# Sums of squares one group later, M products behind the state products, and scores one query behind

## The chip, the cores and the metric

One core of one Trainium2 chip. The metric is the device time of one execution in microseconds; smaller is better.

## What is computed

One layer of a hybrid encoder block over 1024 tokens of width 1024: attention and a bidirectional Mamba-2 mixer side by side, gates, then an expert mixer (PEER) whose experts are picked by product keys. Two places matter here. In the Mamba-2 mixer each chunk of 128 tokens gets, per group of 8 heads, a product with a decay matrix, a product with the running state, and then a norm over the whole width:

```python
y_diag = jnp.einsum('bgrcls,bcsgrp->bclgrp', cb[:, :, None] * Lmat, X)
y_off = jnp.einsum('bclgn,bcgrpn,bgrcl->bclgrp', Cc, states, jnp.exp(A_cs))
...
y = y_f + y_b + xh * d_skip.astype(jnp.float32).reshape(G, R)[:, :, None]
return rmsnorm(y * jax.nn.silu(z), ssd_norm_w)
```

In PEER every token gets 16 queries (8 heads, two halves); each is scored against 128 keys, and the 16 best are kept:

```python
q = (xt @ w_query).reshape(T, PEER_HEADS, 2, PEER_D_HALF)
s1 = jnp.einsum('thd,hkd->thk', q[:, :, 0], keys1).astype(jnp.float32)
v1, i1 = lax.top_k(s1, PEER_TOPK)
```

## The kernel before

The kernel is one long program in stages. Large matmuls are done as three passes over rounded high parts and remainders (`mm3`, L209 to L211), so one product over 8 tiles of the contraction is 24 matmuls. In most stages a scheduler of the framework orders each engine's instructions and gives out the buffers when the program is built; on the chip each engine then runs its own list strictly in that order.

**The state-space stage** (from `discretize`, L689, to L868). A first loop over chunks 7 to 1 makes the backward states. The second loop over chunks 0 to 7 calls `outputs(c, ...)`, which handles two groups of 8 heads, g = 0 and 1. Per group: POOL writes four masked tiles `r0h, r0l, r1h, r1l` (L796); PE multiplies them (L802), ACT takes the exponential `E` (L804); POOL and DVE build `M` from `cb` and `cu` (L806, L809) and multiply it with `E` (L811); PE multiplies `M` with the chunk's tokens `xk` into a PSUM tile `y` (L815, "the products with M"). PE spreads the decays over 128 rows (L820), ACT copies them to `de` (L824), PE multiplies the states `St` and `Sb` (L830, "the state products"). DVE joins all to `yt` (L832 to L840), multiplies it with the gate `zt` loaded from DRAM (L843); the result is stored, ACT squares it into `zt` (L845), and PE sums the squares over the rows with four matmuls (L849) into `oq`. After the second group ACT copies the sums to `ysum` (L852).

`oq` and `cu` share one PSUM bank: `cu` is its second half, and DVE's step L809 reads it. `oq`, `y` and four other short-lived tiles of a chunk come from the same three banks (`C1`, tag `pb`). `step(FSTEP)` ends a group with two pieces of other work that is ready, the filler: columns of the input projection, later of the attention's up projection. A piece is 24 or 12 matmuls into the single bank `w`, with weights split by ACT (L179) and POOL (L180). The scheduler spreads filler between the group's steps on PE. The filler is used up before the last chunks.

**The query loop** (L1112 to L1120) is behind the attention's and mixer's output product. For each of 16 query tiles m: 24 matmuls with 384 columns give the first 384 tokens' queries in PSUM, ACT copies them to `q` (L1083), PE scores them against the keys with three matmuls (`score`, L1093), ACT copies the scores to `s` (L1094), and DVE picks the 16 best of each of three blocks (`top`, L1101 to L1105). The normalising of the other 640 tokens runs beside it (`normed`, L1031, L1033, and its splits at L179 and L180). After the loop the order on PE, DVE and POOL is written out by hand: routing of the three blocks (`route`, with an exponential at L1180), hidden products of the experts (`hb`, gelu at L1459), the other tokens' queries, and then the expert stages up to the end.

Of the kernel before, what the change touches and what calls it, by code (L numbers as in the profile page):

```python
# [10 lines left out]
F32 = mybir.dt.float32  # L11
# [13 lines left out]
NB = -(-TB // 128)  # L25
# [99 lines left out]
def block(ctx, tc, A, out, dbg=None):  # L125
    nc = tc.nc
    dbg = dbg or {}
    V, ACT, PE, POOL = nc.vector, nc.scalar, nc.tensor, nc.gpsimd
# [22 lines left out]
    one = ka[:, K_ONE:K_ONE + 128]  # L151
# [150 lines left out]
    r = rstd(p0, acc, S, 1.0 / D)  # L302
# [313 lines left out]
    def C1():  # L616
        return psC.tile([128, 512], F32, name="pb", bufs=4 - NW)
# [15 lines left out]
    ss = pool("ss")  # L633
# [50 lines left out]
    def step(k):  # L684
        nonlocal steps
        for _ in range(min(k, steps - KEEP)):
            steps -= 1
            next(filler, None)
# [53 lines left out]
    def states(c, d, xc, xk):  # L742
        o = C1()
        for g in range(2):
            PE.transpose(o[:, g * 128:(g + 1) * 128], xc[:, 8 + g], ident)
        bk = ss.tile([128, 256], F32, name="bk")
        ACT.copy(bk, o[:, :256])
        xd = ss.tile([128, D], F32, name="xd")
        POOL.tensor_tensor(xd.rearrange("p (h d) -> p h d", h=16), xk.rearrange("p (h d) -> p h d", h=16),
                           dd[:, c, 16 * d:16 * d + 16].unsqueeze(2).to_broadcast([128, 16, 64]), op=OP.mult)  # L750
        o = C2()
        for g in range(2):
            PE.matmul(o[:, g], lhsT=bk[:, g * 128:(g + 1) * 128], rhs=xd[:, g * 512:(g + 1) * 512], start=True, stop=True)
        return o

    def advance(src, o, c, d):
        dst = ss.tile([128, D], F32, name="St", bufs=2)
        if src is None:
            ACT.copy(v2(dst), o)
            return dst  # L760
        t = ss.tile([128, D], F32, name="adv")
        V.tensor_tensor(t.rearrange("p (h d) -> p h d", h=16), src.rearrange("p (h d) -> p h d", h=16),
                        tot[:, c, 16 * d:16 * d + 16].unsqueeze(2).to_broadcast([128, 16, 64]), op=OP.mult)
        V.tensor_tensor(v2(dst), o, v2(t), op=OP.add)
        return dst

    def outputs(c, xc, xk, Sf):
# [22 lines left out]
        for g in range(2):  # L790
# [9 lines left out]
            for j in range(2):  # L800
                for i, (w, r) in enumerate(R):
                    PE.matmul(o[:, j], lhsT=w, rhs=r[:, 4 * j:4 * j + 4], start=(i == 0), stop=(i == 3))  # L802
            E = ss.tile([128, 8, 128], F32, name="E")
            ACT.activation(E.rearrange("p (s h) l -> p s (h l)", s=2), o, AF.Exp)  # L804
            M = ss.tile([128, 8, 128], F32, name="M", bufs=2)
# [3 lines left out]
                V.scalar_tensor_tensor(M[:, r], cu[:, g], dt[:, c, 8 * g + r:8 * g + r + 1], M[:, r],  # L809
                                       op0=OP.mult, op1=OP.add)  # L810
            V.tensor_tensor(M, M, E, op=OP.mult)  # L811
            y = C1()
            for r in range(8):
                h = 8 * g + r
                PE.matmul(y[64 * (r % 2):64 * (r % 2) + 64, (r // 2) * 128:(r // 2 + 1) * 128],  # L815
                          lhsT=xk[:, h * 64:(h + 1) * 64], rhs=M[:, r], start=True, stop=True, skip_group_check=True)
            od = C2()
            for d in dirs:
                for j in range(4):
# [6 lines left out]
            for d in dirs:  # L826
                st = (Sf, Sb)[d]
                for j in range(4):
                    hs = slice((8 * g + 2 * j) * 64, (8 * g + 2 * j + 2) * 64)
                    PE.matmul(of[:, d, j * 128:(j + 1) * 128], lhsT=st[:, hs], rhs=xc[:, 10 + g],  # L830
                              start=True, stop=True, skip_group_check=True)
            V.tensor_tensor(de[:, ds], of[:, ds], de[:, ds], op=OP.mult)  # L832
            yt = ss.tile([128, 4, 128], F32, name="yt", bufs=2)
            ytf = yt.rearrange("p a l -> p (a l)")
# [3 lines left out]
            for j in range(4):  # L838
                m = 4 * g + j
                V.scalar_tensor_tensor(yt[:, j], xc[:, m], cols[:, C_DS + m:C_DS + m + 1], yt[:, j], op0=OP.mult, op1=OP.add)  # L840
            zt = ss.tile([128, 4, 128], F32, name="zt")
            nc.sync.dma_start(zt, z_d[:, 4 * g:4 * g + 4, cl_(c)])
            V.tensor_tensor(yt, yt, zt, op=OP.mult)  # L843
            nc.sync.dma_start(y_d[:, 4 * g:4 * g + 4, cl_(c)], yt)
            ACT.activation(zt, yt, AF.Square)  # L845
            if g == 0:
                qr = slice(32 * (c // 2), 32 * (c // 2) + 32)
            for j in range(4):
                PE.matmul(oq[qr, :128], lhsT=one[:, 0:32], rhs=zt[:, j], start=(g == 0 and j == 0),  # L849
                          stop=(g == 1 and j == 3))  # L850
            step(FSTEP)
        ACT.copy(ysum[qr, (c % 2) * 128:(c % 2) * 128 + 128], oq[qr, :128])  # L852

    def cl_(c):
        return slice(c * 128, (c + 1) * 128)
# [9 lines left out]
    for c in range(8):  # L865
        xc, xk = tokens(c)
        outputs(c, xc, xk, Sf)
        if c < 7:  # L868
            Sf = advance(Sf, states(c, 0, xc, xk), c, 0)
    step(10 ** 6)  # L870
    ss.release()
    psC.release()
# [234 lines left out]
    def new_q():  # L1107
        return sp.tile([128, S], F32, name="q", bufs=2)

    norm = normed(ends[1], accs[1])  # L1110
    next(norm)
    for m in range(16):  # L1112
        q = new_q()
        for _ in query(weights(A["wq"][m], 8), q, CUTS[:1]):
            pass
        if m % 2 or not m:
            next(norm)
        s = score(m, q, range(NB))
        for b in range(NB):
            top(m, s[:, b], b)  # L1120

    psD.release()
    psE = pool("psE", space=PSUM)
# [743 lines left out]
```

## Time and profile before

| | us |
|---|---|
| runs of the kernel | 3949.39, 3956.99, 3957.73; median 3956.99 |
| the profiled execution | 3962.2 |
| its span in the trace | 3960.4 |
| state-space outputs, first to last L802/L849 | 690 to 1043 of the span |
| query loop | 1284 to 1386 of the span |

The profile is one execution on the chip. Engines: PE is the matmul engine, PEld its weight loads, DVE the vector engine, ACT the scalar engine, POOL GpSimd, SP the queue of DMA issues. A line such as L849 is the line of the kernel that issued the instruction. "Idle before" an instruction is time in which its engine stood still, with what ended it. Matmuls with 32-bit operands stand as two rows each in the trace's counts, so four of them read x8. [...]

### The profile page before, as it was taken

Reading aid. Unit: us, or ns where it says so; the run is one execution under the profiler, and the core shown is the slowest. Engines: PE = TensorE matmul, PEld = TensorE weight load, DVE = VectorE, ACT = ScalarE, POOL = GpSimd, SP = SyncE. Lnnn points to the kernel's source line nnn. Section 1 sums busy time; section 2 is a strip of 40 time slices with the busy share of each in tenths; the row PEclk is TensorE's granted clock in tenths of the full one; section 3 lists DMA queues with packets and bytes.
Section 4 is the critical chain, followed back from the end, with each engine's and each line's share of the span. In section 5 each row is a group of like instructions: output and inputs, shape, how many; then the busy total and the mean of one; then the engine's idle time right before and its main releaser. Section 6 shows DMA issues by size and latency. Waiting matters only on the chain. (4 is left out here: it accounts for less than half of the span.)

```text
span 3960.4 us, 61117 instructions
## 1 busy us (share of the span) xinstructions
PE 3631.6 (92%) x22927; PEld 3189.8 (81%) x22927; DVE 2574.5 (65%) x5289; ACT 1356.3 (34%) x2672; POOL 1803.3 (46%) x1526
## 2 busy tenths in 40 slices
PE   7999999988889899999889798699999999999998
PEld 4777767766679799987678698697888999888997
DVE  5788831457672678787875567594447898545556
ACT  5455532223323433322236465222122222222222
POOL 3111122566454567778775456444443444444200
PEclk9999999998899999999999899799999999999999
DMA  5111134233375258877767778888887888888632
GB/s 197 47 46 48 55 117 144 92 106 101 122 241 168 94 201 317 311 284 258 244 231 273 264 265 320 310 300 303 322 323 246 295 297 292 310 317 314 236 117 81
DMA packets 387064, 852.32 MB, mean 215 GB/s; under 512 B 32720, under 2 KB 146896, under 8 KB 384080
## 3 DMA queue, kind: packets, MB, share of 16 engines
q1 hardware_dynamic: 276176, 445.72, 32.9%
q0 software_dynamic: 110592, 402.70, 28.7%
q8 instruction: 180, 2.95, 0.3%
q14 instruction: 116, 0.95, 0.1%
HBM read 739.70 MB, written 108.59 MB: 214 GB/s over the span
## 5 line engine op out<-in xcount | busy, mean ns | idle before, releaser
L209 PE MATMUL hb<-ah,wh 128*128 128x320 f32 x2048 | 653.2, 319 | 24.0 <-ACT a L1459 24.0
L211 PE MATMUL hb<-ah,wl 128*128 128x320 f32 x2048 | 641.1, 313 | 9.7 <-POOL wl L199 9.7
L210 PE MATMUL hb<-al,wh 128*128 128x320 f32 x2048 | 639.9, 312 | 0.0
L1282 POOL DMA_INDIRECT br<-u,bidx x384 | 370.3, 964 | 369.0 <-DVE br L1314 243.2
L199 POOL TENSOR_TENSOR wl<-wr,wh 128x512 fp32r<-128x512 f32 x269 | 352.9, 1317 | 397.3 <-ACT wh L198 367.6
L209 PE MATMUL pb<-Wh,vh 128*128 128x320 f32 x1536 | 477.1, 317 | 57.1 <-ACT Wh L1689 33.7
L180 POOL TENSOR_TENSOR wl<-wr,wh 128x512 fp32r<-128x512 f32 x172 | 233.0, 1358 | 615.5 <-ACT wh L179 450.6
L1282 POOL DMA_INDIRECT br<-v,ixt x384 | 376.8, 981 | 267.5 <-PE gx L1361 155.1
L210 PE MATMUL pb<-Wl,vh 128*128 128x320 f32 x1536 | 481.4, 314 | 1.7 <-DVE Wl L1692 1.6
L211 PE MATMUL pb<-Wh,vl 128*128 128x320 f32 x1536 | 479.6, 313 | 0.0
L1314 DVE SCALAR_TENSOR_TENSOR br<-br,gx 128x1024 f32<-128x1024 f32 x384 | 454.0, 1214 | 8.6 <-DMA br<-u,bidx 6.3
L209 PEld LDWEIGHTS hb<-ah,wh 128*128 128x128 f32 x2048 | 391.9, 191 | 52.7 <-ACT a L1459 28.2
L211 PEld LDWEIGHTS hb<-ah,wl 128*128 128x128 f32 x2048 | 390.7, 191 | 11.3 <-POOL wl L199 10.3
L210 PEld LDWEIGHTS hb<-al,wh 128*128 128x128 f32 x2048 | 391.5, 191 | 0.0
L1722 DVE TENSOR_TENSOR acc<-acc,pb 128x320 f32<-128x320 f32 x491 | 230.6, 485 | 222.2 <-PE pb L211 221.0
L179 ACT CAST vh<-vr 128x512 fp32r<-128x512 f32 x256 | 151.1, 618 | 649.8 <-PE pb L210 449.0
L209 PEld LDWEIGHTS pb<-Wh,vh 128*128 128x128 f32 x1536 | 289.6, 190 | 84.4 <-ACT Wh L1689 37.0
L198 ACT CAST wh<-wr 128x512 fp32r<-128x512 f32 x288 | 178.2, 619 | 397.8 <-PE hb L210 188.2
L210 PEld LDWEIGHTS pb<-Wl,vh 128*128 128x128 f32 x1536 | 292.5, 190 | 5.4 <-DVE Wl L1692 4.3
L211 PEld LDWEIGHTS pb<-Wh,vl 128*128 128x128 f32 x1536 | 292.9, 191 | 0.4
L1478 DVE TENSOR_TENSOR quad<-io,rig 128x1024 f32<-128x1024 f32 x160 | 191.7, 1221 | 139.1 <-PE pb L1493 78.0
L180 DVE TENSOR_TENSOR vl<-vr,vh 128x512 fp32r<-128x512 f32 x256 | 203.9, 797 | 76.8 <-ACT vh L179 76.8
(367 smaller groups left out, 8218.4 us busy)
## 6 DMA issues: line engine op xcount, KB each, us to landing
wr<-uT SPq DMA_DIRECT2D x256, 256.0 KB, 3.9
vr<-v SPq DMA_DIRECT2D x256, 256.0 KB, 5.3
G_d<-stg SPq DMA_DIRECT2D x20, 2048.0 KB, 11.7
gt<-G_d SPq DMA_DIRECT2D x42, 960.0 KB, 6.5
a_d<-a SPq DMA_DIRECT2D x85, 320.0 KB, 5.3
a<-a_d SPq DMA_DIRECT2D x85, 320.0 KB, 5.9
wr<-wi SPq DMA_DIRECT2D x84, 256.0 KB, 2.7
sq<-adaT SPq DMA_DIRECT2D x32, 512.0 KB, 3.8
```

The source lines that it names most:

```text
L179: ACT.copy(hi, src)
L180: (eng or POOL).tensor_tensor(lo, src, f32(hi), op=OP.subtract)
L198: ACT.copy(h, raw)
L199: late.append(lambda: (eng or POOL).tensor_tensor(w, raw, f32(h), op=OP.subtract))
L209: PE.matmul(o, lhsT=wh, rhs=xh, start=first, stop=False)
L210: PE.matmul(o, lhsT=wh, rhs=xl, start=False, stop=False)
L211: PE.matmul(o, lhsT=wl, rhs=xh, start=False, stop=last)
L1282: POOL.indirect_dma_start(out=r, out_offset=None, in_=A[tab], in_offset=bass.IndirectOffsetOnAxis(ap=idx, axis=0))
L1314: V.scalar_tensor_tensor(v2(r), v2(r), 1.0, hrow[0], op0=OP.mult, op1=OP.mult, accum_out=a[:, s:s + 1])
L1478: V.tensor_tensor(x, iota.unsqueeze(1).unsqueeze(1).to_broadcast([128, 2, 4, 128]), ig[:, 0:2, t:t + 4].unsqueeze(3).to_broadcast([128, 2, ...
L1722: V.tensor_tensor(acc[:, m, js], acc[:, m, js], o, op=OP.add)
```

## The change

Three things move; no operation is added or taken away. (1) The four matmuls that sum a group's squares are put on a list, and are issued one group later, behind the next group's decay-matrix product; the copy to `ysum` goes with the second group's. (2) The products with M stand behind the decays and the state products. (3) In the query loop a tile's scores and top picks stand behind the next query's matmuls. `zt` gets a second buffer, since the squares live longer.

```diff
--- before.py
+++ after.py
@@ -800,6 +800,8 @@
             for j in range(2):
                 for i, (w, r) in enumerate(R):
                     PE.matmul(o[:, j], lhsT=w, rhs=r[:, 4 * j:4 * j + 4], start=(i == 0), stop=(i == 3))
+            if squares_of:
+                add_squares()
             E = ss.tile([128, 8, 128], F32, name="E")
             ACT.activation(E.rearrange("p (s h) l -> p s (h l)", s=2), o, AF.Exp)
             M = ss.tile([128, 8, 128], F32, name="M", bufs=2)
@@ -809,11 +811,6 @@
                 V.scalar_tensor_tensor(M[:, r], cu[:, g], dt[:, c, 8 * g + r:8 * g + r + 1], M[:, r],
                                        op0=OP.mult, op1=OP.add)
             V.tensor_tensor(M, M, E, op=OP.mult)
-            y = C1()
-            for r in range(8):
-                h = 8 * g + r
-                PE.matmul(y[64 * (r % 2):64 * (r % 2) + 64, (r // 2) * 128:(r // 2 + 1) * 128],
-                          lhsT=xk[:, h * 64:(h + 1) * 64], rhs=M[:, r], start=True, stop=True, skip_group_check=True)
             od = C2()
             for d in dirs:
                 for j in range(4):
@@ -829,6 +826,11 @@
                     hs = slice((8 * g + 2 * j) * 64, (8 * g + 2 * j + 2) * 64)
                     PE.matmul(of[:, d, j * 128:(j + 1) * 128], lhsT=st[:, hs], rhs=xc[:, 10 + g],
                               start=True, stop=True, skip_group_check=True)
+            y = C1()
+            for r in range(8):
+                h = 8 * g + r
+                PE.matmul(y[64 * (r % 2):64 * (r % 2) + 64, (r // 2) * 128:(r // 2 + 1) * 128],
+                          lhsT=xk[:, h * 64:(h + 1) * 64], rhs=M[:, r], start=True, stop=True, skip_group_check=True)
             V.tensor_tensor(de[:, ds], of[:, ds], de[:, ds], op=OP.mult)
             yt = ss.tile([128, 4, 128], F32, name="yt", bufs=2)
             ytf = yt.rearrange("p a l -> p (a l)")
@@ -838,18 +840,24 @@
             for j in range(4):
                 m = 4 * g + j
                 V.scalar_tensor_tensor(yt[:, j], xc[:, m], cols[:, C_DS + m:C_DS + m + 1], yt[:, j], op0=OP.mult, op1=OP.add)
-            zt = ss.tile([128, 4, 128], F32, name="zt")
+            zt = ss.tile([128, 4, 128], F32, name="zt", bufs=2)
             nc.sync.dma_start(zt, z_d[:, 4 * g:4 * g + 4, cl_(c)])
             V.tensor_tensor(yt, yt, zt, op=OP.mult)
             nc.sync.dma_start(y_d[:, 4 * g:4 * g + 4, cl_(c)], yt)
             ACT.activation(zt, yt, AF.Square)
-            if g == 0:
-                qr = slice(32 * (c // 2), 32 * (c // 2) + 32)
-            for j in range(4):
-                PE.matmul(oq[qr, :128], lhsT=one[:, 0:32], rhs=zt[:, j], start=(g == 0 and j == 0),
-                          stop=(g == 1 and j == 3))
+            squares_of.append((oq, c, g, zt))
             step(FSTEP)
-        ACT.copy(ysum[qr, (c % 2) * 128:(c % 2) * 128 + 128], oq[qr, :128])
+
+    squares_of = []
+
+    def add_squares():
+        oq, c, g, zt = squares_of.pop(0)
+        qr = slice(32 * (c // 2), 32 * (c // 2) + 32)
+        for j in range(4):
+            PE.matmul(oq[qr, :128], lhsT=one[:, 0:32], rhs=zt[:, j], start=(g == 0 and j == 0),
+                      stop=(g == 1 and j == 3))
+        if g:
+            ACT.copy(ysum[qr, (c % 2) * 128:(c % 2) * 128 + 128], oq[qr, :128])
 
     def cl_(c):
         return slice(c * 128, (c + 1) * 128)
@@ -867,6 +875,7 @@
         outputs(c, xc, xk, Sf)
         if c < 7:
             Sf = advance(Sf, states(c, 0, xc, xk), c, 0)
+    add_squares()
     step(10 ** 6)
     ss.release()
     psC.release()
@@ -1107,6 +1116,11 @@
     def new_q():
         return sp.tile([128, S], F32, name="q", bufs=2)
 
+    def tops_of(m, q):
+        s = score(m, q, range(NB))
+        for b in range(NB):
+            top(m, s[:, b], b)
+
     norm = normed(ends[1], accs[1])
     next(norm)
     for m in range(16):
@@ -1115,9 +1129,10 @@
             pass
         if m % 2 or not m:
             next(norm)
-        s = score(m, q, range(NB))
-        for b in range(NB):
-            top(m, s[:, b], b)
+        if m:
+            tops_of(m - 1, q0)
+        q0 = q
+    tops_of(15, q0)
 
     psD.release()
     psE = pool("psE", space=PSUM)
```

The lists below are the orders on an engine, one row an instruction (x8: eight in a row), with buffer numbers where rows would read alike; "..." leaves out filler and other rows. Names left of the arrow are written, right of it read.

On PE, in the state-space stage, chunk 2, before: `dec` are the decays, `St` and `Sb` the states, `zt` the squares.

```order
L802 MATMUL pa_6208<-r1l_6206,mr_4557 128x512
L820 MATMUL pa_6239<-dec_6196,kb_4555 128x128 x8
L830 MATMUL pa_6250<-xc_6173,St_6169 128x128 x3
L815 MATMUL pb_6230<-M_6219,xk_6184 64x128 x8
L830 MATMUL pa_6250<-xc_6173,St_6169 128x128
L830 MATMUL pa_6250<-xc_6173,Sb_6198 128x128 x4
...
L802 MATMUL pa_6352<-r0h_6344,mr_4557 128x512
L849 MATMUL pb_6189<-zt_6267,ka_60 32x128 x4
L802 MATMUL pa_6352<-r0l_6346,mr_4557 128x512
...
L849 MATMUL pb_6189<-zt_6411,ka_60 32x128 x4
```

The same place now, up to the next chunk's first transposes (lines of the changed kernel: L817 decays, L827 states, L832 products with M, L857 squares):

```order
L817 MATMUL pa_6230<-dec_6191,kb_4555 128x128 x8
L827 MATMUL pa_6241<-xc_6168,St_6164 128x128 x4
L827 MATMUL pa_6241<-xc_6168,Sb_6193 128x128 x4
L832 MATMUL pb_6250<-M_6219,xk_6179 64x128 x8
...
L802 MATMUL pa_6348<-r1l_6346,mr_4557 128x512
L857 MATMUL pb_6184<-zt_6267,ka_60 32x128 x4
L817 MATMUL pa_6374<-dec_6191,kb_4555 128x128 x8
...
L745 MATMUL pb_6484<-ka_60,xc_6168 128x128 x2
L770 MATMUL pb_6511<-xc_6498 128x128 x2
L857 MATMUL pb_6184<-zt_6411,ka_60 32x128 x4
```

All eight state products now stand ahead of the products with M. The first group's squares stood behind 21 filler matmuls and five of the second group's L802; now they stand behind 48 filler matmuls and all eight L802. The second group's stood behind 24 filler matmuls; now there are 22 of them behind two fillers and the products with M, and the next chunk's transposes and small products (L745, L770) besides.

On PE at the head of the query loop, before: `pb<-bh,wh` and its neighbours are the query's 24 matmuls, `rstd` is the norm of the other tokens.

```order
L1093 MATMUL pb<-keys,q 128x128
L237 MATMUL pa<-rstd_160_10142,ka 128x160 x4
L1093 MATMUL pb<-keys,q 128x128 x2
L209 MATMUL pb<-bh,wh 128x384
...
L1093 MATMUL pb<-keys,q 128x128 x3
```

Now:

```order
L237 MATMUL pa<-rstd_160_10142,ka 128x160 x4
L209 MATMUL pb<-bh,wh 128x384
...
L1102 MATMUL pb<-keys,q 128x128 x3
L209 MATMUL pb<-bh,wh 128x384
...
L1102 MATMUL pb<-keys,q 128x128 x6
```

Six matmuls of the second query stand ahead of L237 now, the first scores behind the rest of them, and so on to the last: the scores of tiles 14 and 15 are issued together behind the last query.

On ACT, behind the query loop, before and then now (`rg` is the routing's exponential, `a` the gelu):

```order
L198 CAST wh<-wr 128x512
L1180 ACT_TABLE_LOAD
L1180 ACTIVATE rg<-rg 128x128
L1459 ACT_TABLE_LOAD
L1459 ACTIVATE a<-hb 128x320 x2
```

```order
L198 CAST wh<-wr 128x512
L1474 ACT_TABLE_LOAD
L1474 ACTIVATE a<-hb 128x320
L1195 ACT_TABLE_LOAD
L1195 ACTIVATE rg<-rg 128x128
L1474 ACT_TABLE_LOAD
L1474 ACTIVATE a<-hb 128x320
```

One gelu now stands ahead of the exponential, at the price of a third table load.

## Rows read from the trace of the kernel before

**Rows 1.** The page, part 1: busy us, share of the span, instructions.

```profile
PE 3631.6 (92%) x22927; PEld 3189.8 (81%) x22927; DVE 2574.5 (65%) x5289; ACT 1356.3 (34%) x2672; POOL 1803.3 (46%) x1526
```

**Rows 2.** Windows: length, busy of PE, PEld, DVE, ACT, POOL, PEclk, DMA.

```profile
690.00:1043.00 353.00, 305.57 (x1655) 234.91 (x1653) 202.50 (x316) 108.22 (x156) 204.11 (x107) 0.90 0.30 95
1284.00:1400.00 116.00, 98.78 (x585) 93.37 (x581) 81.84 (x483) 50.25 (x89) 57.27 (x44) 0.97 0.30 99
```

**Rows 3.** PE's waits from 690 to 890: us, times, longest.

```profile
PE pb L849 <- ACT zt L845: 13.1, 8, 2.2
PE pb L815 <- DVE M L811: 3.6, 4, 1.0
```

**Rows 4.** PE's waits from 890 to 1043.

```profile
PE pb L849 <- ACT zt L845: 8.5, 5, 3.5
PE pb L815 <- DVE M L811: 5.5, 2, 3.6
```

**Rows 5.** PE in time, the stage's waits: start, us, what, [idle before].

```profile
711.26 1.06 PE L849 MATMUL pb<-zt,ka 128*32 128x128 f32 x8 [2.18 <-ACT zt L845]
782.02 1.06 PE L849 MATMUL pb<-zt,ka 128*32 128x128 f32 x8 [1.46 <-ACT zt L845]
800.06 1.09 PE L815 MATMUL pb<-M,xk 128*64 128x128 f32 x16 [1.00 <-DVE M L811]
831.55 1.06 PE L849 MATMUL pb<-zt,ka 128*32 128x128 f32 x8 [0.93 <-ACT zt L845]
```

**Rows 6.** Windows of 20 us in the stage, columns as in rows 2.

```profile
700.00:720.00 20.00, 16.88 (x88) 13.05 (x87) 10.64 (x16) 4.30 (x8) 12.32 (x7) 0.91 0.22 72
760.00:780.00 20.00, 18.92 (x111) 15.61 (x112) 8.59 (x16) 4.87 (x7) 11.01 (x6) 1.00 0.31 102
960.00:980.00 20.00, 16.79 (x92) 12.53 (x91) 16.03 (x23) 7.98 (x12) 10.05 (x6) 0.91 0.42 133
```

**Rows 7.** PE in time, second group of chunk 2.

```profile
819.58 2.05 PE L820 MATMUL pa<-dec,kb 16*128 16x128 f32 x16
821.56 1.16 PE L830 MATMUL pa<-xc,St 128*128 128x128 f32 x8
822.83 1.09 PE L815 MATMUL pb<-M,xk 128*64 128x128 f32 x16
```

**Rows 8.** DVE and ACT in time, chunk 2.

```profile
797.36 2.64 DVE L811 TENSOR_TENSOR M<-M,E 128x1024 f32<-128x1024 f32 x1 [0.20 <-ACT E L804]
811.72 2.16 DVE L809 SCALAR_TENSOR_TENSOR M<-pb,dt,M 128x128 f32<-128x128 f32 x8 [1.93 <-PE pb L849]
826.38 0.69 DVE L835 TENSOR_TENSOR yt<-pb,de 128x512 f32<-128x512 f32 x1
830.87 0.63 ACT L845 ACTIVATE zt<-yt 128x512 f32<-128x512 f32 x1 [2.58 <-DVE yt L843]
```

**Rows 9.** Query loop: PE's waits from 1290 to 1390, and one period in time.

```profile
PE pb L1093 <- ACT q L1083: 14.1, 15, 1.0
PE pb L1093 <- DMA keys<-keys: 3.1, 1, 3.1
...
1306.51 0.94 PE L1093 MATMUL pb<-keys,q 128*128 128x128 f32 x6 [0.91 <-ACT q L1083]
1312.53 0.94 PE L1093 MATMUL pb<-keys,q 128*128 128x128 f32 x6 [0.91 <-ACT q L1083]
```

**Rows 10.** Window in the query loop, where the other tokens are normalised.

```profile
1300.00:1320.00 20.00, 16.77 (x100) 15.82 (x101) 15.76 (x83) 16.32 (x28) 17.56 (x13) 1.00 0.24 80
```

**Rows 11.** Behind the query loop: DVE's last top and routing, PE's wait, the window.

```profile
1386.66 0.49 DVE L1101 MAX8 best<-s 128x8 f32<-128x128 f32 x2 [2.17 <-ACT s L1094]
1400.80 0.29 DVE L1179 TENSOR_TENSOR rg<-rs 128x128 f32<-128x128 f32 x1
1403.23 0.64 PE L209 MATMUL hb<-ah,wh 128*128 128x320 f32 x1 [3.04 <-ACT a L1459]
1400.00:1410.00 10.00, 6.96 (x30) 6.77 (x29) 9.06 (x17) 3.29 (x6) 6.38 (x4) 0.66 0.21 79
```

## The prediction

> **What bounds the kernel now.** I read the page first: PE is busy for 92% of the span [rows 1], so a wait of PE is time, and work moved elsewhere is not. Then the windows by stage: in the state-space stage PE is busy 305.6 of 353.0 us at a mean granted clock of 0.90, in the query loop's stretch 98.8 of 116.0 [rows 2]. No other engine comes near: DVE has 202.5 and POOL 204.1 of the 353. So both stages are PE's list with holes in it. Third, who ends the holes. From 690 to 890 it is the squares eight times, 13.1 us, and the products with M four times, 3.6 us [rows 3]; from 890 to 1043 the squares five times, 8.5 us, and M twice, 5.5 us [rows 4]. In the query loop PE waits 15 times for the copy of the query that it has just finished, 14.1 us, and once 3.1 us at the start [rows 9]. Last, the clock: where a squares' wait is 2.18 us long the 20 us window shows 0.91, where it is 1.46 us it shows 1.00 [rows 5, 6]. [...] Five windows of the stage show 0.91; the first and the last stand there.
>
> **The change, part by part.** All sums are against the profiled execution, 3962.2 us; it is 5.2 us above the median of the runs.
>
> *Squares of chunks 0 to 3.* After the products with M, DVE and ACT need from 826.38 to 831.50, 5.1 us, until the squares are there [rows 8]. Before, PE had 24 filler matmuls and four to five state products behind those products; a filler matmul takes 0.23 us (831.55 less the wait of 0.93, less the end of the state products at 822.83 + 1.09 + 1.16, over 24) [rows 5, 7]. Now a first group has 48 of them, 11 us, and eight L802: its wait goes. A second group has 22, 5.1 us, and the next chunk's four transposes and small products, with the joining of `de` already done: its wait goes or shrinks to a few tenths. I take -13.1; the bound is -9.4, if the four second groups keep the shortest wait shown, 0.93.
>
> *Products with M.* In a first group five state products more now stand ahead of them, 5 x 2 rows x 0.145 = 1.45 us (1.16 over 8 rows) [rows 7]; the longest wait was 1.00 [rows 3, 5]. I take -3.6.
>
> *A wait that the change adds.* DVE's eight steps L809 read `cu`, which lies in the bank into which the squares are summed, and they wait for the squares of the group before: the row shows 1.93 us idle until L849 [rows 8]. The squares now come 48 filler matmuls later, right ahead of the decays. Behind them DVE has 2.16 us of L809 and 2.64 us of L811 (as slow as it is shown, beside POOL), 4.8 us [rows 8]. PE has the decays, 2.05, the state products, 2 x 1.16, and two filler matmuls, 0.46: 4.8 us [rows 7]. Queued behind the waiting DVE step are `de` and `yt`, which nothing needs sooner. It comes out even, so I take 0; between 0 and +1 us in each of four groups. [...]
>
> *Clock in chunks 0 to 3.* Three windows of 0.91 there lose 3 x 1.8 = 5.4 us; with the waits of 2 us gone the level should hold. Between 0 and -5.4; I take -4.
>
> *Chunks 4 to 6.* The squares' waits are 8.5 less the last one, 3.5 (it stands at the end of the stage, and nothing is put ahead of it): 5.0 us. Two windows at 0.91 are 3.6 us more. Filler comes in pieces of 12 there, and DVE is busier (16.0 of 20 in the last window) [rows 4, 6]. Between 0 and -8.6; I take the middle, -4.3. The last chunk has no filler, its M wait (the longest of rows 4, 3.6) and its squares stay.
>
> *Query loop.* A period is 6.02 us, of it 0.91 the wait and 0.94 the scores [rows 9]; so 24 matmuls take 4.17, 0.174 each. With the scores a query behind, the copy has a whole query's time; only behind the last query a few tenths are left. -14.1. At the start six matmuls of the second query fill 1.0 of the 3.1 us; L237 behind them still waits for the norm. -1.0. What comes next in time is POOL: 17.56 us busy in 20 us [rows 10], which is 5.3 us in a period that shrinks to 5.1, over some four periods; its splits of the weights are what PE would wait for. +1 (0 to +2).
>
> *Behind the loop.* Two tiles' top picks now stand behind the last scores in place of one. DVE's picks and routing take from 1386.66 to 1400.80 there, and PE waits 3.04 us for a gelu that stands behind that routing's exponential on ACT; the window is at 0.66 [rows 11]. Three picks more stand ahead of it, at most a period's work; but one gelu now goes ahead of the exponential, and PE can work on one product longer. Between +3, the wait doubled, and -6.4 (the wait gone, and with it the 3.4 us that 0.66 costs in 10 us). I take 0.
>
> Sum: -13.1 - 3.6 + 0 - 4 - 4.3 - 14.1 - 1.0 + 1 + 0 = -39.1 us. Past each place the engines' orders are the old ones, and no wait there is on a time that stays fixed, so I let the gain run through to the end. 3962.2 - 39.1 = 3923.1 for an execution like the profiled one, 3918 against the median.
>
> **Rivals.**
> 1. *More of it comes.* The low clock and the late chunks' waits all go (-1.4, -4.3) and so does the stall behind the loop (-6.4): 3906. For it: every one of these holes has a length in the rows. Against it: DVE and POOL are loaded in just these windows.
> 2. *Only the query loop pays.* The state-space stage turns its waits into the one on M above, or into other engines' lateness. Then -14.1 - 1.0 + 1 remains: 3943. For it: the cover of 4.8 us is exactly as long as the work. Against it: it needs the whole 25 us of the stage, some 3 us in every group, where the count gives tenths.
> 3. *Slower, by banks.* `oq` is now held into the next chunk, and a chunk's short-lived tiles share three banks. If the next chunk's first transposes had to wait for the squares and `ysum`, every one of seven chunk borders would stand still for the chain behind the products with M, 5.1 us plus 1.06 for the squares, and lose 1.8 us of clock: 7 x 8.0 = 56 us against 39 gained, 3974. It decides from 5.6 us a border on. Against it: in the new order those transposes stand ahead of the squares, so that a bank was found for them.
> 4. *It is absorbed.* A later stage holds PE for other engines and gives nothing on: 3950 to 3957. Against it: everything there is shifted together.
>
> **How the numbers follow.** The forecast, both parts at about their counted size (3908 to 3932), has 0.62; rival 1 0.15, rival 2 0.13, rival 3 0.05, rival 4 0.05. The likeliest is 3918. The range takes in rival 1 with some of the 8 us by which the runs shown differ, and rival 2: 3900 to 3944; rivals 3 and 4 are left out. About 0.2%, 8 us, is what a measurement of this kernel can tell from no change. Faster than that: the forecast, rivals 1 and 2, 0.90. Within it: most of rival 4, 0.04. Slower: rival 3 and a mishap of the kind, 0.06.
>
> **What would show it.** In the profile after, PE's waits for `zt` should be gone but for the end of the stage and some tenths in second groups, those for M too up to the last chunks; the stage's windows should show 1.00 up to 880. PE's wait for `q` should be one of tenths in place of 15, the loop's period 5.1 us. The stage should be some 25 us shorter, the loop 14. I am wrong if PE waits for M in each second group, if the transposes at chunk borders wait for a bank, or if the two stages shrink as said and the end does not come earlier by as much.

## The result, and the profile after

The changed kernel takes 3919.9 us (median of 6 runs, 3914.1 to 3937.8) against 3957.4 for the kernel before: ratio 0.9911, interval 0.9885 to 0.9936. The medians differ by 37.5 us; the ratio, by which the experiments below are read too, makes it 35.2. Timed again beside later experiments the ratio was 0.9895 (0.9876 to 0.9913). The forecast was 3918, 39.1 us less. The profiled execution took 3914.1 us, its span is 3912.3, 48.1 less than the span before; some 9 us of that lie ahead of the stage (2.7) or behind the gelu's product that ends the loop (6.0), and are not shown to be the change's.

Part 1 of the page of the changed kernel, and the windows that answer to [rows 2] (start and end, us, then busy time of PE, PEld, DVE, ACT, POOL, the granted clock (PEclk) as a share of full speed, the DMA share and GB/s):

```profile
PE 3613.9 (92%) x22927; PEld 3181.2 (81%) x22927; DVE 2573.6 (66%) x5289; ACT 1352.7 (35%) x2671; POOL 1804.6 (46%) x1526
```

```profile
664.00:1017.00 353.00, 319.94 (x1752) 248.00 (x1750) 201.96 (x317) 108.97 (x160) 208.65 (x110) 0.95 0.33 104
1256.00:1372.00 116.00, 106.31 (x664) 104.40 (x663) 95.48 (x502) 54.53 (x101) 69.81 (x52) 0.97 0.34 112
```

In equal lengths of time PE is now busy for 319.9 us in place of 305.6, and for 106.3 in place of 98.8 (the same lengths, not the same work: the stages are shorter now, so neighbouring work falls into them); the clock of the state-space stretch is 0.95 where it was 0.90.

To measure the stage by itself I take it from the start of the last product of the backward loop (L753) to the first product behind the stage. Timeline of PE, kernel before, then the changed one:

```profile
671.09 1.02 PE L753 MATMUL pa<-xd,bk 128*128 128x512 f32 x2
...
1043.13 0.79 PE L209 MATMUL pb<-am,wh 128*128 128x512 f32 x1 [0.35 <-ACT ysum L852]
```

```profile
668.41 1.02 PE L753 MATMUL pa<-xd,bk 128*128 128x512 f32 x2
...
1017.19 0.79 PE L209 MATMUL pb<-am,wh 128*128 128x512 f32 x1 [0.35 <-ACT ysum L860]
```

The end comes 25.9 us earlier, but 2.7 of these were there before the first changed instruction. The stage's own gain is 372.04 - 348.78 = 23.3 us, and in the second profile of the same program 372.04 - 352.90 = 19.1. The forward loop's L753 rows part the stage: chunks 0 to 3 went from 209.2 to 194.3 and 195.9, chunks 4 to 7 from 162.8 to 154.4 and 157.0.

Who ends PE's holes now, chunks 0 to 3 (680 to 880; us in total, times, longest), against [rows 3]:

```profile
PE w L209 <- ACT zg L652: 6.4, 4, 2.1
PE pb L832 <- DVE M L813: 1.2, 2, 0.9
...
PE pb L857 <- ACT zt L847: 0.4, 1, 0.4
```

Squares 13.1 to 0.4, M 3.6 to 1.2, and a wait that was not forecast: the filler's for `zg`, 0.2 before. From 880 to 1020, against [rows 4]:

```profile
PE pb L857 <- ACT zt L847: 14.2, 3, 5.6
PE pb L832 <- DVE M L813: 4.1, 3, 3.6
```

Here the squares' waits did not go; they are fewer and longer, and 8.5 us became 14.2 (11.1 in the second profile).

The query loop on PE: two scores one period apart, and the one long wait for `q` that is left (0.29 us more stands behind the last query).

```profile
1303.82 0.83 PE L1102 MATMUL pb<-keys,q 128*128 128x128 f32 x6
...
1308.65 0.83 PE L1102 MATMUL pb<-keys,q 128*128 128x128 f32 x6
```

```profile
1294.01 0.94 PE L1102 MATMUL pb<-keys,q 128*128 128x128 f32 x6 [2.10 <-ACT q L1092]
```

The period is 4.83 us in place of 6.02. The wait at 1294.01 is read on ACT:

```profile
1292.25 0.83 ACT L1042 ACTIVATE t<-t,mod 128x640 f32<-128x640 f32 x1 [2.85 <-DVE t L1040]
1292.98 0.60 ACT L179 CAST wh<-wr 128x512 fp32r<-128x512 f32 x1
1293.49 0.47 ACT L1092 COPY q<-pb 128x384 f32<-128x384 f32 x1
```

The copy of q stands in ACT's list behind a step of the other tokens' norm, which waits for DVE; once in the loop that is later than PE.

Behind the loop PE, then ACT and DVE, to be held against [rows 11]:

```profile
1361.06 0.64 PE L209 MATMUL hb<-ah,wh 128*128 128x320 f32 x1 [5.52 <-ACT a L1474]
```

```profile
1358.94 0.31 ACT L1195 ACTIVATE rg<-rg 128x128 f32<-128x128 f32 x1 [5.08 <-DVE rg L1194]
```

```profile
1346.15 0.90 DVE L1161 CAST rf<-where 128x256 f32<-128x256 uint32 x1
...
1358.63 0.28 DVE L1194 TENSOR_TENSOR rg<-rs 128x128 f32<-128x128 f32 x1
```

The wait grew from 3.04 to 5.52. Routing (from `rf`) begins on DVE only when two tiles' picks are through, at 1346.15.

From this gelu's product (1403.23 before, 1361.06 after) to the end of the span no code differs, and yet the 14 profiles shown below have between 2547.6 and 2570.9 us there. The changed kernel itself has 2551.2 and 2547.6, and 2570.9 when only the last tile of the loop is altered. Part of this is likely the chip: the three longest, 2562.6 to 2570.9 (the last tile's picks earlier, and the kernels with both edits and ACT from chunk 4 or the gate on POOL), come from one chip, on which the kernel before took 3970.8 us in place of 3957.4 to 3963.6 elsewhere. The eight from another chip lie between 2547.6 and 2558.4, in an order that the edits do not explain. So I read each experiment at two marks, the stage's length and the time of the gelu's product, besides the ratio.

| kernel | ratio to before (interval) | chunks 0-3 | chunks 4-7 | gelu's product at |
|---|---|---|---|---|
| before | 1 | 209.2 | 162.8 | 1403.2 |
| the change | 0.9911 (0.9885 to 0.9936) | 194.3 | 154.4 | 1361.1 |
| the change again | 0.9895 (0.9876 to 0.9913) | 195.9 | 157.0 | 1367.0 |
| query loop alone | 0.9963 (0.9950 to 0.9976) | 210.4 | 161.4 | 1388.0 |
| state-space stage alone | 0.9948 (0.9933 to 0.9963) | 195.8 | 157.1 | 1382.9 |
| squares alone | 0.9973 (0.9960 to 0.9986) | 196.6 | 160.6 | 1385.8 |
| M alone | 1.0004 (0.9991 to 1.0017) | 212.5 | 159.0 | 1401.1 |
| squares by DVE | 0.9885 (0.9867 to 0.9903) | 187.0 | 163.2 | 1368.0 |
| squares ahead of M's products | 0.9901 (0.9882 to 0.9920) | 195.0 | 152.9 | 1365.4 |
| both | 0.9878 (0.9859 to 0.9896) | 186.8 | 154.8 | 1354.5 |
| both, ACT from chunk 4 | 0.9877 (0.9856 to 0.9899) | 186.7 | 150.5 | 1351.9 |
| both, gate on POOL | 0.9898 (0.9884 to 0.9912) | 186.7 | 155.2 | 1359.4 |
| last tile's picks earlier | 0.9887 (0.9872 to 0.9902) | 194.4 | 154.5 | 1360.1 |
| all together | 0.9876 (0.9855 to 0.9896) | 186.7 | 150.6 | 1350.8 |

The columns of chunks are differences of L753 rows (the last ends at the first product behind the stage), the last column is the start of the row that waits for the gelu. Four profiles hold the stage of the changed kernel as it is (the change, the change again, state-space stage alone, last tile's picks earlier): they differ by 1.5 us in the first column of chunks and by 2.7 in the second, and differences of that size between other rows are not read.

### The profile page after: what moved, and what is told of

Same layout as the page of the kernel before. It is cut to its first block, busy times and chain, and to the rows that moved or that the text cites. A ratio compares the mean times of both kernels' runs of the same rounds, so it can differ in the third digit from the quotient of the medians.

```text
span 3912.3 us, 61114 instructions
## 1 busy us (share of the span) xinstructions
PE 3613.9 (92%) x22927; PEld 3181.2 (81%) x22927; DVE 2573.6 (66%) x5289; ACT 1352.7 (35%) x2671; POOL 1804.6 (46%) x1526
## 5 line engine op out<-in xcount | busy, mean ns | idle before, releaser
L1297 POOL DMA_INDIRECT br<-v,ixt x384 | 377.5, 983 | 271.5 <-PE gx L1376 159.0
L209 PEld LDWEIGHTS pb<-Wh,vh 128*128 128x128 f32 x1536 | 289.2, 190 | 81.9 <-ACT Wh L1704 32.3
## 6 DMA issues: line engine op xcount, KB each, us to landing
G_d<-stg SPq DMA_DIRECT2D x20, 2048.0 KB, 10.7
```

What stands on the lines that cost most here:

```text
L209: PE.matmul(o, lhsT=wh, rhs=xh, start=first, stop=False)
L1297: POOL.indirect_dma_start(out=r, out_offset=None, in_=A[tab], in_offset=bass.IndirectOffsetOnAxis(ap=idx, axis=0))
```

## The experiments

**The parts by themselves.** Four kernels, each with one part of the change on the kernel before. The query loop alone:

```diff
-        s = score(m, q, range(NB))
-        for b in range(NB):
-            top(m, s[:, b], b)
+        if m:
+            tops_of(m - 1, q0)
+        q0 = q
+    tops_of(15, q0)
```

> The kernel before, with only the query loop changed (scores and picks one query later). Theory 1 (the parts add up, nothing later takes the gain away): in the trace the loop is 13 to 14 us shorter, PE's waits for q are gone; the wait for the gelu behind the loop grows from 3.0 to about 5.5 us as in the changed kernel; so the time is 11 to 13 us under the kernel before, ratio 0.9967 to 0.9972. Theory 2 (the query loop's gain is kept only because the state-space stage ends earlier, or it is lost in the later stages): under 6 us, ratio above 0.9985.

14.6 us less (3959.0 x 0.0037; 9.5 to 19.8): theory 1, a little over the 11 to 13 us expected. From L237 at the head of the loop (1289.85) to the gelu's product it is 98.1 us, before 112.0. The stall behind the loop comes with it:

```profile
1387.95 0.63 PE L209 MATMUL hb<-ah,wh 128*128 128x320 f32 x1 [5.51 <-ACT a L1465]
```

The state-space part alone (the changed kernel with the loop as it was):

> The changed kernel with the query loop of the kernel before. Theory 1: the state-space stage ends 26 us earlier as in the changed kernel, the loop's period stays at 6.0 us, the wait behind the loop at about 3.0 us; 24 to 26 us under the kernel before, ratio 0.9934 to 0.9940. Theory 2 (later stages swallow part of it): under 18 us, ratio above 0.9955.

20.6 us less (14.6 to 26.5), the stall behind the loop 3.03. The two alone make 35.2, together the change was measured at 35.2 and, the second time, at 41.6 (3962.7 x 0.0105): within intervals of some 5 to 10 us each they add up, and nothing later is seen to swallow them. The size is under what I expected here, since I had taken the 2.7 us ahead of the stage for its gain.

Within the stage, the squares alone:

```diff
+            if squares_of:
+                add_squares()
...
-            for j in range(4):
-                PE.matmul(oq[qr, :128], lhsT=one[:, 0:32], rhs=zt[:, j], start=(g == 0 and j == 0),
-                          stop=(g == 1 and j == 3))
+            squares_of.append((oq, c, g, zt))
```

> The kernel before with the squares one group later alone; the products with M keep their place ahead of the state products. Theory 1 (the squares' waits and the low clock behind them are most of the stage's gain): PE's waits for zt in chunks 0 to 3 fall from 13.1 us to under 1.5, those for M stay at some 3 to 5 us, the clock is 1.00 there; the stage ends 19 to 23 us earlier, ratio 0.9942 to 0.9952. Theory 2 (the two moves need each other: with M's products early, DVE's steps that wait for the squares make PE wait for M in first groups too): the waits for M grow to 10 us and more, the stage ends at most 12 us earlier, ratio above 0.997.

and the products with M alone, squares in place:

```diff
-            y = C1()
...
             of = C2()
...
+            y = C1()
...
             V.tensor_tensor(de[:, ds], of[:, ds], de[:, ds], op=OP.mult)
```

> The kernel before with the products with M behind the state products alone; the squares keep their place. Theory 1 (a move of M alone only shifts the wait): PE waits for M no more in chunks 0 to 3 (-3.6 us), but the squares then have 20 filler matmuls ahead of them in place of 24 and four to five state products, 1.6 us less, so their waits grow by about 1 us in seven groups; between 4 us faster and 8 us slower, ratio 0.999 to 1.002. Theory 2 (the parts of the prediction's sum stand each for itself): the M term alone, -3.6 us and the late chunks' M waits -2, ratio 0.9985 with the waits for the squares unchanged at 13 us.

PE's waits from 680 to 885, squares alone, then M alone:

```profile
PE pb L817 <- DVE M L813: 5.0, 6, 1.4
PE w L209 <- ACT zg L652: 4.4, 4, 1.3
```

```profile
PE pb L849 <- ACT zt L845: 13.8, 5, 3.2
PE pb L830 <- DVE M L811: 0.9, 1, 0.9
```

Squares alone: 10.7 us less (5.5 to 15.8), in the profile's stage 14.8: the squares' waits are 0.4, but M's rise to 5.0. By the waits that is theory 1, by the ratio theory 2, and the stage's gain lies between the two. M alone: 1.6 us more (3.6 less to 6.7 more), its own wait goes from 3.6 to 0.9, the squares' are 13.8 in five waits of up to 3.2 in place of eight up to 2.2, and chunks 0 to 3 take 3.3 us more. So M's move alone is worth nothing that the runs can tell, and is worth something (4 to 8 us of the profiles' stage) once the squares are out of the way: the terms of my sum for squares and for M are not independent.

**The new wait for `zg`.** In the trace of the changed kernel the chain is seen on three engines, in chunk 2. PE, ACT, DVE:

```profile
797.78 0.50 PE L209 MATMUL w<-hh,wh 128*128 128x512 f32 x1 [1.56 <-ACT zg L652]
```

```profile
796.11 0.63 ACT L847 ACTIVATE zt<-yt 128x512 f32<-128x512 f32 x1 [3.37 <-DVE yt L845]
796.64 0.60 ACT L179 CAST wh<-wr 128x512 fp32r<-128x512 f32 x1
797.15 0.58 ACT L652 COPY zg<-w 128x512 f32<-128x512 f32 x1
```

```profile
791.65 3.70 DVE L842 SCALAR_TENSOR_TENSOR yt<-xc,cols,yt 128x128 f32<-128x128 f32 x4
795.38 0.69 DVE L845 TENSOR_TENSOR yt<-yt,zt 128x512 f32<-128x512 f32 x1
```

The copy that frees the filler's only bank stands on ACT behind the square, and the square waits for DVE. Before, PE had its own wait for that square and came to the next filler later. If that is so, the square taken by DVE itself frees ACT:

```diff
-            ACT.activation(zt, yt, AF.Square)
+            V.tensor_tensor(zt, yt, yt, op=OP.mult)
```

> The changed kernel with the square taken by DVE (product of yt with itself) in place of ACT; PE's order in chunks 1 to 3 stays word for word. It tests the new wait of 6.4 us of the filler for zg. Theory 1 (ACT copies zg late because the square ahead of it in ACT's list waits for DVE's yt): PE's waits for zg in chunks 0 to 3 fall from 6.4 us to under 1.5; the stage ends 4 to 7 us earlier than in the changed kernel, ratio 0.989 to 0.9905. Theory 2 (the copy of zg is late by itself, since PE has ended the filler just then, or DVE's 0.6 us more in each of 16 groups takes it all back): the waits for zg stay above 4 us or come back as waits for M; ratio 0.991 to 0.993.

PE's waits, 680 to 880, all that there are, then the longest from 880 to 1020:

```profile
PE w L210 <- DVE am L180: 3.6, 2, 2.7
PE w L209 <- ACT am L179: 1.5, 1, 1.5
PE pb L832 <- DVE M L813: 1.2, 2, 0.9
```

```profile
PE w L209 <- DVE mh L677: 10.1, 3, 4.7
PE pb L857 <- DVE zt L847: 6.1, 3, 3.4
```

The wait for `zg` is gone, and chunks 0 to 3 take 187.0 us in place of 194.3 and 195.9. Theory 1 holds for the cause. But chunks 4 to 7 pay it back, 163.2 us: the filler there waits for DVE's product with the gate, `mh`. The ratio, 0.9885, is within the interval of the changed kernel.

**The added wait of M for the squares.** The prediction set it at 0. Taking it away, by issuing the sums behind the state products:

```diff
-            if squares_of:
-                add_squares()
             E = ss.tile([128, 8, 128], F32, name="E")
...
+            if squares_of:
+                add_squares()
             y = C1()
```

> The changed kernel with the sums of squares issued behind the state products (and behind DVE's steps on cu in the order of the program) in place of behind the decay-matrix product. It takes away DVE's wait for the squares ahead of M (42.7 us in 8 waits) and gives the squares of chunks 4 to 6 more time. But PE's order changes: the filler that stood ahead of the products with M in second groups now stands behind them. Theory 1 (the added wait of M for the squares costs nothing, as predicted; the cover ahead of M is what counts): the waits for zt in chunks 4 to 6 fall from 10.8 us to under 4, and the waits for M do not grow by more than 2 us: 4 to 8 us faster than the changed kernel, ratio 0.989 to 0.990. Theory 2 (products with M right behind the state products have no cover): PE waits 0.5 to 1.5 us for M or E in each second group, and the stage is 0 to 8 us longer than the changed kernel's, ratio 0.991 to 0.993.

DVE's waits from 680 to 1020, changed kernel, then this one:

```profile
DVE M L811 <- PE pb L857: 42.7, 8, 9.4
```

```profile
DVE M L811 <- ACT E L804: 50.3, 10, 11.0
```

DVE's wait for the squares has only stood in place of one for E, which needs the same eight L802 of PE. The stage takes 347.9 us, with the wait 348.8 and 352.9: its price, in this order of PE's list, is 0 within 5 us. PE's waits for squares in chunks 4 to 7 fall to 2.4, and 13.3 us of waiting for `mh` come instead. Neither theory's time is borne out; the ratio is that of the changed kernel.

**What holds the late chunks.** Both edits together:

> The last two edits together: squares taken by DVE and summed behind the state products. Theory 1 (zg and the late squares are separate holes): the gains of the two add up, some 8 to 14 us under the changed kernel, ratio 0.987 to 0.989. Theory 2 (DVE becomes the late engine in chunks 4 to 6, where it is at 106 of 155 us): no better than the better of the two alone.

Chunks 0 to 3 as with the first edit, chunks 4 to 7 as in the changed kernel; the stage, 341.6 us, is shorter than with either edit alone (350.2 and 347.9), and the gelu's product comes 6.6 and 12.6 us earlier than in the changed kernel's two profiles: theory 1 by these marks, while the ratios can't tell it from theory 2. The waits for `mh` are 16.4 us. Two kernels ask whether DVE's load makes them. ACT takes the squares again from chunk 4 on:

```diff
-            V.tensor_tensor(zt, yt, yt, op=OP.mult)
+            if c < 4:
+                V.tensor_tensor(zt, yt, yt, op=OP.mult)
+            else:
+                ACT.activation(zt, yt, AF.Square)
```

> The kernel with both edits (squares summed behind the state products, squares taken by DVE), but from chunk 4 on ACT takes the squares again. Theory 1 (DVE is the late engine in chunks 4 to 6, and its 0.6 us for a square is part of that lateness): the filler's waits for mh fall from 16.4 us to 12 or less, chunks 0 to 3 stay at 187 us and chunks 4 to 7 come to 150 to 153 us from 154.8: 2 to 4 us faster than with both edits, ratio 0.9865 to 0.988. Theory 2 (the filler's waits there come from where filler stands in PE's list, not from DVE's load): chunks 4 to 7 stay at 154 to 157 us.

The waits for `mh` fall to 13.8, less than I expected, but chunks 4 to 7 to 150.5: theory 1 in the time, half of it in the wait (the last kernel below, with the same stage, has 10.7). And the gate's product leaves DVE:

```diff
-                V.tensor_tensor(part1[m][:, js], o, gt, op=OP.mult)
+                ACT.copy(part1[m][:, js], o)
+                POOL.tensor_tensor(part1[m][:, js], part1[m][:, js], gt, op=OP.mult)
```

> The kernel with both edits, and the filler's last step in chunks 4 to 6, the product with the gate that DVE does into mh, is split: ACT copies the sums out of PSUM, POOL multiplies. It frees the filler's only bank without DVE. Theory 1 (PE's waits for mh are the wait for DVE's list, in which the step stands behind M): they fall from 16.4 us to under 5, chunks 4 to 7 come to 142 to 150 us from 154.8; 5 to 12 us faster than with both edits, ratio 0.985 to 0.9865. Theory 2 (POOL, with 1.3 us more in each of 12 pieces, brings its masked tiles later, and DVE's steps beside POOL grow slower still): waits of L802 for POOL grow by as much; no gain or a loss, ratio 0.9875 or more.

PE's waits from 880 to 1020:

```profile
PE pb L858 <- DVE zt L848: 15.8, 4, 9.3
PE pa L803 <- POOL mh L678: 2.4, 1, 2.4
PE w L209 <- ACT mh L677: 1.7, 3, 0.8
```

The filler's wait is gone (1.7), and the squares wait 15.8 in its place; the chunks take 155.2 as against 154.8. That is theory 2 in the time, though not quite by its way. Parted at chunk 6's L753 rows, chunks 4 to 6 did gain, 122.9 us for 127.7, and the last chunk, in which no filler is left, lost it again, 32.3 for 27.1. So the wait for the bank had a price where the filler stands. That the bank was only the place where PE met DVE's lateness fits the squares' 15.8 us, but is not shown, and why the last chunk grew stays open.

**The stall behind the loop.** The scores and picks of tile 14 go ahead of the last query's matmuls:

```diff
+        if m == 15:
+            tops_of(14, q0)
         for _ in query(weights(A["wq"][m], 8), q, CUTS[:1]):
...
-        if m:
+        if 0 < m < 15:
```

> The changed kernel, but the scores and picks of tile 14 stand ahead of the last query's matmuls again, so that only one tile's picks stand behind the last scores. It tests why the wait for the gelu behind the loop grew from 3.0 to 5.5 us. Theory 1 (DVE's picks of tile 14, 3.5 us, stand ahead of the routing whose exponential holds the gelu back on ACT): that wait is 3.0 us again, PE waits about 0.9 us for the copy of q of tile 14; 1.5 us faster, ratio 0.988 to 0.991, no difference that the runs can show. Theory 2 (the wait is longer because PE comes to it earlier by another way, the gelu's and exponential's order on ACT): it stays at 5.0 to 5.5 us.

```profile
1360.10 0.64 PE L209 MATMUL hb<-ah,wh 128*128 128x320 f32 x1 [3.08 <-ACT a L1476]
```

3.08 us again: theory 1. From L237 to this row it is 96.2 us in place of 98.1 and 97.6, the 1.5 us expected; the runs can't show it (0.9887).

**The change once more**, as it is, beside the three kernels with DVE's squares, with the sums behind the state products, and with both:

> The changed kernel as it is, timed again on the chip of the next three. Theory 1 (the two parts, which measured -20.6 and -14.6 us alone, add up): 33 to 41 us under the kernel before, ratio 0.9896 to 0.9917. Theory 2 (the first measurement caught a favourable chip): under 28 us, ratio above 0.993.

0.9895, 41.6 us less (34.5 to 49.1): theory 1, at the upper end of what it gave, and its second profile is what the marks are compared with throughout.

**All together**: sums behind the state products, squares by DVE up to chunk 3, tile 14's picks early.

> The edits that shortened their place in the trace put together: squares summed behind the state products, taken by DVE in chunks 0 to 3 and by ACT from chunk 4 on, and the picks of tile 14 ahead of the last query's matmuls. Theory 1 (holes of PE removed in a place come off the end): the stage takes 336 to 339 us in place of 349 to 353 in the changed kernel, the wait for the gelu is 3.0 us; 12 to 17 us under the changed kernel, ratio 0.985 to 0.988. Theory 2 (the later stages, which move 300 GB/s, give a gain of this size back): stage and loop as said, but the ratio stays at 0.988 to 0.991, that of the changed kernel.

The combined kernel has its stage at 337.3 us, the stall at 3.08, and the gelu's product 10.2 and 16.2 us ahead of the changed kernel. Its ratio is 0.9876 (0.9855 to 0.9896) against 0.9911 and 0.9895: the lowest of all, but its interval overlaps theirs. Behind the mark this profile has 2558.1 us, 7 more than the first profile of the change and inside the 11 us by which that stretch differs on one chip. Whether the later stages give part of it back stays open.

## Why the prediction was right, point by point

The time, the sign and the mechanism were right: both parts pay, and the gain comes off the end. That the total came within some 4 us of the forecast is partly luck: chunks 0 to 3 and 4 to 6 gave less than forecast, the last chunk gave what the sum had not put down, and the loop gave more, which the longer stall behind it took back.

- *Squares of chunks 0 to 3*, -13.1: measured -12.7. *M*, -3.6: -2.4. *Clock*, -4 (a window at 0.91 counted as 1.8 us, 0.09 of its 20; in the kernel before the one from 700 has 1.00 in each us up to 712, and 0.50 from 713 to 716): in the first profile no 20 us window from 680 to 860 is under 1.00, so -5.4; in the second the window from 840 has 0.91, so -3.6. (The wait of 1.46 us that the prediction sets beside a clock of 1.00 ends at 782.02, in the window behind the one shown there; that one has 1.00 too.) The three make -20.5 and -18.7, and I had -20.7. The clock of 1.00 did not last up to 880: the window from 860, into which chunk 4 now falls, has 0.83.
- *What I missed there*: chunks 0 to 3 gained 14.9 and 13.3 us, not 20.7. The step that failed is in "squares of chunks 0 to 3: its wait goes". I asked what PE has ahead of the squares, not what stands behind the square on ACT; the wait came back as 6.4 us for `zg`, and the DVE-square kernel takes it away. -12.7 - 2.4 - 5.4 + 6.2 = -14.3, and with the second profile's clock -12.5.
- *Chunks 4 to 6*, -4.3: measured +0.1 and +2.6 (123.9 before, 124.0 and 126.5 now). The middle of the range was taken, and the row that spoke against it, DVE at 16.0 of 20 us, was named and not weighed. And the term counted the squares' waits and left out the longest wait of these chunks, the filler's for `mh` (6.9 us, the first line below; the 20 us from 900 on, in which it stands, have a granted clock of 0.67). In the changed kernel that wait is 1.0 us, but the squares' went from 5.0 to 10.8 and 7.8. All PE's waits between these chunks' L753 rows make 15.9 us before, 15.6 and 15.9 now: their owner changed, not their sum.
- *The last chunk "stays"*: it went from 38.9 to 30.4 us. Its waits for M and squares did stay (3.6 and 3.35), but a third one went, the second of these lines of the waits from 885 to 1045 of the kernel before, neither of which I had taken up:

```profile
PE w L209 <- DVE mh L677: 6.9, 1, 6.9
...
PE pa L802 <- DVE St L764: 4.6, 1, 4.6
```

It belongs to M's move: with that alone it is 0.8 us, with the squares alone 5.5 in two waits. The rest is the clock: the last chunk before, then now, with PE's busy time first and its granted clock third from the end:

```profile
1004.21:1043.13 38.92, 24.78 (x122) 17.40 (x120) 23.11 (x42) 8.73 (x14) 13.27 (x7) 0.66 0.19 58
```

```profile
986.76:1017.19 30.43, 20.83 (x120) 14.63 (x120) 18.51 (x38) 8.73 (x14) 13.21 (x7) 0.82 0.22 64
```

The same products take 20.8 us in place of 24.8. Against the forecast chunks 0 to 3 are +5.8 and +7.4 us, 4 to 6 +4.4 and +6.9, the last -8.5 and -8.4: the stage came out at -23.3 and -19.1 for -25.

- *Added wait for the squares*, 0: borne out within 5 us by the kernel without it (a stage of 347.9 us, with it 348.8 and 352.9), in which PE's order changes too. No run parts `oq` and `cu`; what the traces show is DVE's wait itself, 42.7 us in eight waits in the changed kernel, and that it cost nothing that these runs can tell.
- *Query loop*, -14.1 + 1 + 0, and -1.0 at its start: from L237 to the gelu's product -14.0 and -14.5, and the wait at the head of the loop went from 3.1 (ahead of the first scores, ended by the keys' DMA) to 1.8 (ahead of L237, for the norm). 14 periods took 84.7 us, from the second tile's scores on, and now 70.4, from the first's; in these is the wait at 1294.01 (that period is 2.6 longer), which stands where I had put POOL's +1 but is made by DVE and ACT. A period is 4.83, not 5.1. The prediction took the row's length of 0.94 us for the scores, but the next query's matmuls start before it ends: from start to start it was 0.69 us, and is 0.58 now that the scores wait for nothing; and the query's 24 matmuls take 4.25 up to the next scores, where up to the wait they took 4.42. Behind the loop it was +2.5, near the upper end of the +3 to -6.4 given.
- *The gain runs through*: the parts add up in the runs, and the mark at the gelu's product is 42.2 and 36.2 us earlier, of which 2.7 and 0.8 were there ahead of the stage.
- *Rivals*: 2 and 3 did not come, since both parts pay and no transpose at a chunk's border waits for a bank. Rival 1 asked for chunks 4 to 6 and for the stall behind the loop; neither paid. Rival 4 did not come either: the time fell by about as much as the parts.

## What to carry to other kernels

When a consumer is put off, look at the in-order list of the engine that makes its input: whatever stands behind that producer is now the first to be late (here ACT's copy to `zg`, for which PE waited 6.4 us where it had waited 0.2). Terms for two waits in one chain are not independent (here 10.7 us less and 1.6 more alone, 20.6 less together), so time each move alone before adding them. Count every wait of a stretch, not only the ones that the change aims at: in chunks 4 to 6 the waits changed hands and their sum stayed. And where the rest of the program varies by more than the change, measure at a mark right behind it, and compare times of one chip.

## What the runs showed of the hardware

In these two traces DVE's steps slow down beside POOL by their operands: one line goes from 348 to 769 ns, another has 344 and 342. Groups by line on DVE (mean ns of one behind the comma), kernel before, 1025 to 1045, and POOL's busy time in that stretch (0.00, the fourth number from the end):

```profile
L809 DVE SCALAR_TENSOR_TENSOR M<-pb,dt,M 128x128 f32<-128x128 f32 x8 | 2.2, 344 | 1.2 <-PE pb L849 1.2
...
L840 DVE SCALAR_TENSOR_TENSOR yt<-xc,cols,yt 128x128 f32<-128x128 f32 x4 | 1.1, 348 | 0.0
```

```profile
1025.00:1042.00 17.00, 9.93 (x49) 7.59 (x48) 6.68 (x17) 2.77 (x4) 0.00 (x0) 0.50 0.16 46
```

The same two lines in the changed kernel from 860 to 1010, where POOL is busy 91 of 150 us:

```profile
L842 DVE SCALAR_TENSOR_TENSOR yt<-xc,cols,yt 128x128 f32<-128x128 f32 x28 | 19.8, 769 | 0.2
L811 DVE SCALAR_TENSOR_TENSOR M<-pb,dt,M 128x128 f32<-128x128 f32 x64 | 17.4, 342 | 9.3 <-PE pb L857 5.3 <-POOL M L808 4.0
```

One operation and one size: with `cu` from PSUM it keeps its 342 ns, with both tensors from SBUF it goes from 348 to 769. The means could hide that the one never met POOL, so here is each in a single place of the changed kernel: L842 while POOL stands still (from 903.43 to 910.18), and L811 while POOL writes a masked tile (`r0h`, L796, from 917.70 to 919.60).

```profile
907.69 1.14 DVE L842 SCALAR_TENSOR_TENSOR yt<-xc,cols,yt 128x128 f32<-128x128 f32 x4
917.77 2.16 DVE L811 SCALAR_TENSOR_TENSOR M<-pb,dt,M 128x128 f32<-128x128 f32 x8 [1.67 <-POOL M L808]
```

L842 alone takes 1.14 us for four steps, and L811 beside POOL 2.16 for eight, as without it. At the second longest wait for squares the two engines stand side by side; PE, DVE, POOL of the changed kernel:

```profile
894.53 1.70 PE L857 MATMUL pb<-zt,ka 128*32 128x128 f32 x7 [5.22 <-ACT zt L847]
```

```profile
887.04 6.05 DVE L842 SCALAR_TENSOR_TENSOR yt<-xc,cols,yt 128x128 f32<-128x128 f32 x4
```

```profile
886.53 2.34 POOL L796 TENSOR_TENSOR r0l<-kb,avl 128x1024 fp32r<-128x1024 f32 x1
888.84 1.94 POOL L796 TENSOR_TENSOR r1h<-kb,avh 128x1024 fp32r<-128x1024 f32 x1
890.74 1.94 POOL L796 TENSOR_TENSOR r1l<-kb,avl 128x1024 fp32r<-128x1024 f32 x1
```

Four steps of 0.3 us take 6.05 beside three tiles of POOL, and end 0.4 us after the last of them. The first three take 1.98 us each, the second and third begin 0.1 us behind the end of a tile, and the fourth, begun 0.1 us behind the last tile, takes 0.34: as if no more than one step got in at each border between two tiles. Three more lines of the changed kernel's stretch from 860 to 1010 go with it, each beside the same step of the kernel before from 1025 to 1045: L837, with `y` from PSUM, has 690 ns, before 691; L845 and L813, with both tensors from SBUF, have 1089 and 1917 ns, before 691 and 1225. Why the operands decide is not shown. These slow steps are the likely root of the late squares and of the 3.37 us on ACT above (the four steps of L842 ahead of it took 3.70 us, with POOL busy for 3.02 of them), and of why one edit after another in chunks 4 to 7 mostly moved the wait. That was read from the traces; no kernel was run in which those four steps are one, or POOL is kept off them.
